# Moving join's scratch into shared tiles, adding a fourth buffer for low parts, and moving one part's token differences to VectorE

## The chip, the cores and the metric

The kernel runs on one core of a Trainium2 chip. The metric is the device time of one execution in microseconds. Three runs of the kernel before took 2678.21, 2679.01 and 2679.69 us; their median, 2679.01 us, is the time that the change is compared with.

## The reference, cut to what matters

A two-layer decoder trunk on 1024 tokens of 1024 channels, all float32. The first layer mixes tokens by the RWKV-7 recurrence with 16 heads of 64 channels, the second by sliding-window attention; each is followed by a squared-ReLU MLP of width 4096. The change touches the first layer alone, and the buffers of the weights of all layers:

```python
xx = token_shift(h) - h                       # differences of neighbouring tokens
xs = h[None] + xx[None] * mu[:, None, None, :]
r, k, v = jnp.einsum('nbtc,ncd->nbtd', xs[:3], w_rkv)   # xw, xa, xg feed the low-rank branches
...
def step(S, inp):                             # wkv7: state S per head, 64 x 64
    r_t, w_t, k_t, v_t, a_t, b_t = inp
    sa = jnp.einsum('bhvk,bhk->bhv', S, a_t)
    S = S * w_t[:, :, None, :] + sa[..., None] * b_t[:, :, None, :] + v_t[..., None] * k_t[:, :, None, :]
    y = jnp.einsum('bhvk,bhk->bhv', S, r_t)
    return S, y
```

## The kernel before, in words

**Products in three matmuls.** Every float32 operand of a large product is split into a high part (a cast to fp32r, ScalarE, L129) and a low part (source less high part, L130, VectorE unless `split` is given another engine). `mm3` then issues three matmuls, L134 to L136. Weights come from HBM into `wr` (5 buffers), their high part goes to `wh` (4 buffers) and their low part to `wl` (3 buffers, `WL = 3`); a [128, 512] tile is 2 KB a partition. In `prod_n` (tokens on the output's partitions) `wl` is read by L135, in `prod_t` (channels there) by L136. A buffer is free for the next weight when the last matmul that reads it is done.

**The first layer's projections** run in three parts of 256, 256 and 512 tokens (`PARTS`). For the first two parts `steps` (L336) takes the differences `dx` of neighbouring tokens, four instructions of [128, 512] on GpSimd (L344); `shifted` then makes each mixed input by one VectorE instruction a channel tile (L353, into one of 3 `relu` buffers), a high part on ScalarE, and a low part, which in the first part is GpSimd's for all 8 tiles (`POOLED`).

**The recurrence** runs in 16 units (8 blocks of 128 tokens by 2 groups of 8 heads), each of two chunks of 64 tokens. A unit is prepared (`prep`, `inner`), two 32 x 32 triangular systems per head are solved on GpSimd (`solve`, L680 and L682) and come back by DMA into `RT`; `join` builds the blocks between them: VectorE transposes `RT`'s blocks into columns 0 to 31 of `XT` (L700), TensorE multiplies (L705), ScalarE copies the product to a tile of its own, `AT` (L707), and TensorE multiplies again (L711). `chunks` then does for each chunk: L743, the right side `pb` (ScalarE, L745), L748, the solve's product L752, its copy into `SV` (VectorE, L754), the state's product L757, the sum `sn` (VectorE, L759), the decayed state (L762 for the next chunk, L763 for `state`) and L766. `AT`, `pb` and `sn` are one buffer each, 1 KB a partition.

**Order.** A scheduler of the framework lays out each engine's instructions from the program's order, priorities and its own cost model; the recurrence is given priority over the products beside it. Each engine then runs its list strictly in order: an instruction that waits holds up everything behind it on its engine. So a buffer count changes the whole list, not only the waits. With the first half's 8 units done, the first half goes through the output projection (`mix_out`) and the MLP, beside which the other 8 units run; attention and the second layer follow.

Of the kernel before, what the change touches and what calls it, by code (L numbers as in the profile page):

```python
# [10 lines left out]
F32 = mybir.dt.float32  # L11
# [3 lines left out]
ALU = mybir.AluOpType  # L15
# [4 lines left out]
P = 128  # L20
# [7 lines left out]
D = 64  # L28
L = 64
TB = 128  # L30
NC = TB // L
GP = 4
# [3 lines left out]
B = 32  # L36
# [7 lines left out]
M2K = 24  # L44
WR = 5
WH = 4
WL = 3
ROWS = 4
STG = 3
RELU = 3  # L50
# [24 lines left out]
class Trunk:  # L75
# [25 lines left out]
    def t(self, pool, tag, shape, dt=F32, bufs=1):  # L101
        return pool.tile(shape, dt, tag=tag, name=self.nm(tag), bufs=bufs)
# [162 lines left out]
    def weight(self, ap, shape, gain=None):  # L265
# [3 lines left out]
        nc.sync.dma_start(raw, ap)  # L269
        hi, lo = self.t(self.mp, "wh", shape, F32R, WH), self.t(self.mp, "wl", shape, F32R, WL)  # L270
        if gain is None:
# [64 lines left out]
    def steps(self, hT, n):  # L336

        self.dx = None
        if n > 256:
            return  # L340
        self.dx = []
        for k in range(0, KT, 2):
            d = self.m2k().bitcast(F32).rearrange("p (k t) -> p k t", t=n)
            self.nc.gpsimd.tensor_tensor(d, hT[0][:, k:k + 2, 0:n], hT[0][:, k:k + 2, 1:], ALU.subtract)  # L344
            self.dx += [d[:, 0], d[:, 1]]

    def shifted(self, hT, i, n):
# [27 lines left out]
    def lora_out(self, W2, u, off, dst, pt):  # L375
# [7 lines left out]
        for o in range(KT):  # L383
            if o % 4 == 0:
                raw = self.t(self.mp, "wr", [P, 512], F32, WR)
                for r0 in (0, 64):
                    nc.sync.dma_start(raw[r0:r0 + 64], W2[:, o * P:o * P + 512])
                wh, wl = self.t(self.mp, "wh", [P, 512], F32R, WH), self.t(self.mp, "wl", [P, 512], F32R, WL)
                nc.scalar.copy(wh, raw)
# [92 lines left out]
    def project(self, pt, hT, left):  # L482
# [44 lines left out]
        for group in groups:  # L527
            for o in group:
                prod(0, o)
                step(small, next(steps))  # L530
# [6 lines left out]
            for o in group:  # L537
                ps = prod(1, o)
                sq = self.t(self.mp, "relu", [P, 512], F32, RELU)[:, :n]
                nc.scalar.activation(sq, ps, AF.Square, scale=self.col('k_k', o))  # L540
                if last is None:
                    s = self.bank()
                else:
                    squares(*last)
                last = (o, sq)
                step(small, next(steps))
# [146 lines left out]
    def join(self, made):  # L693

        nc = self.nc
        AR, BK, RT, EL, bonus, XT, Xs = made
        n = NQ // 2
        sides = [(hp, self.sides(hp)[1].start, self.sides(hp)[2].start) for hp in range(2)]
        for hp, b, k in sides:
            nc.vector.transpose(XT[b:b + B, :, 0:B], RT[k:k + B, hp, :, 0:B])  # L700
        AT = self.t(self.rp, "AT", [P, n, B], F32)
        ps = self.turn().rearrange("p (q i) -> p q i", i=B)
        for q in range(n):
            for hp, b, k in sides:
                nc.tensor.matmul(ps[k + B:k + L, q], XT[b:b + B, q, B:], XT[b:b + B, q, 0:B], start=True, stop=True)  # L705
        for hp, b, k in sides:
            nc.scalar.copy(AT[k + B:k + L], ps[k + B:k + L, 0:n])  # L707
        ps = self.turn().rearrange("p (q i) -> p q i", i=B)
        for q in range(n):
            for hp, b, k in sides:  # L710
                nc.tensor.matmul(ps[k:k + B, q], AT[k + B:k + L, q], RT[k + B:k + L, hp, q, B:], start=True, stop=True)  # L711
        for hp, b, k in sides:
            nc.scalar.copy(RT[k:k + B, hp, :, B:], ps[k:k + B, 0:n])
        return AR, BK, RT, EL, bonus

    def chunks(self, blk, g, made):

        nc = self.nc
        t = lambda tag, shape, bufs=1, dt=F32: self.t(self.rp, tag, shape, dt, bufs)
        pt, t0 = PART[blk]  # L720
        AR, BK, RT, EL, bonus = made
        SV = t("SV", [P, NC, 2, GP, D])
        sides = [(hp, *self.sides(hp)[1:]) for hp in range(2)]
        heads = [(pi, *x) for pi in range(GP) for x in sides]
        dV = self.dV[pt][t0:t0 + TB, g * GH * D:(g + 1) * GH * D]
        for hp, bs, ks in sides:
            for c in range(NC):
                nc.sync.dma_start(SV[ks, c, hp], dV[c * L:(c + 1) * L].rearrange("l (r h d) -> l h r d", h=2, d=D)[:, hp])
            nc.vector.tensor_copy(SV[bs, 0, hp], self.state[g][bs])
        bv = t("bv", [P, NC, GH, D])  # L730
        nc.sync.dma_start(bv[L:].rearrange("l c h d -> l c (h d)"), dV.rearrange("(c l) d -> l c d", l=L))
        nc.gpsimd.tensor_tensor(bv[L:], bv[L:], bonus[L:].unsqueeze(3).broadcast_to([L, NC, GH, D]), ALU.mult)
        y = t("y", [P, GP, NC, L])

        def bank():
            return self.turn().rearrange("p (h d) -> p h d", d=D)[:, 0:GP]

        S = self.state[g]
        for c in range(NC):
            el = EL[:, :, c].unsqueeze(2).broadcast_to([P, GP, D])  # L740
            ps = bank()
            for pi, hp, bs, ks in heads:
                nc.tensor.matmul(ps[ks, pi], AR[:, hp, pi * NC + c, L:], SV[:, c, hp, pi], start=True, stop=True)  # L743
            pb = t("pb", [P, GP, D])
            nc.scalar.copy(pb, ps)  # L745
            py = bank()
            for pi, hp, bs, ks in heads:
                nc.tensor.matmul(py[bs, pi], SV[:, c, hp, pi], AR[:, hp, pi * NC + c, 0:L], start=True, stop=True)  # L748
            nc.scalar.copy(y[:, :, c], py)
            ps = bank()  # L750
            for pi, hp, bs, ks in heads:
                nc.tensor.matmul(ps[bs, pi], RT[ks, hp, pi * NC + c], pb[ks, pi], start=True, stop=True)  # L752
            for hp, bs, ks in sides:
                nc.vector.tensor_copy(SV[bs, c, hp], ps[bs])  # L754
            ps = bank()
            for pi, hp, bs, ks in heads:
                nc.tensor.matmul(ps[bs, pi], BK[:, pi * NC + c, hp], SV[:, c, hp, pi], start=True, stop=True)  # L757
            sn = t("sn", [P, GP, D])
            nc.vector.tensor_tensor(sn, ps, S, ALU.add)  # L759
            if c < NC - 1:  # L760
                for hp, bs, ks in sides:
                    nc.vector.tensor_tensor(SV[bs, c + 1, hp], sn[bs], el[bs], ALU.mult)  # L762
            nc.vector.tensor_tensor(S, sn, el, ALU.mult)  # L763
            py = bank()
            for pi, hp, bs, ks in heads:
                nc.tensor.matmul(py[bs, pi], SV[bs, c, hp, pi], RT[bs, hp, pi * NC + c], start=True, stop=True)  # L766
            nc.vector.tensor_tensor(y[:, :, c], y[:, :, c], py, ALU.add)
        return y, bv
# [355 lines left out]
```

## Time and profile before

| what | value |
|---|---|
| median of three runs | 2679.01 us |
| the profiled execution | 2679.98 us |
| its span, first to last instruction | 2678.3 us |
| TensorE (PE) busy | 2541.7 us, 95% |
| VectorE (DVE) busy | 1700.6 us, 63% |
| ScalarE (ACT) busy | 1306.1 us, 49% |
| GpSimd (POOL) busy | 621.2 us, 23% |
| mean granted TensorE clock | 0.972 of full speed |

The profile is of one execution. Busy shares are means over stages that differ: in the first 800 us the other engines are nearly as busy as TensorE, after that TensorE hardly ever stops. In the rows below, times are in microseconds from the span's start, "L130" is a line of the kernel, and what stands behind an arrow at a row's end is what ended the idle time before it.

### The profile page before, as it was taken

How to read it: one execution, taken by the hardware profiler on the slowest of the kernel's cores; microseconds unless marked ns; L12 is line 12 of the kernel's file. 1: busy time of each engine (PE TensorE's matmuls, PEld its weight loads, DVE VectorE, ACT ScalarE, POOL GpSimd, SP SyncE). 2: the span in 40 equal slices, each digit the busy share in tenths (PEclk: the TensorE clock that was granted, in tenths of full speed). 3: DMA queues.
4: the chain of work that ended last, by engine and by line, in shares of the span. 5: the costliest groups of instructions: out<-in, count | busy, mean ns of one | idle time of the engine just before them, and what ended most of it. 6: DMA issues, size and time to landing. Idle time of an engine off the chain costs nothing.

```text
span 2678.3 us, 43154 instructions
## 1 busy us (share of the span) xinstructions
PE 2541.7 (95%) x15166; PEld 2054.0 (77%) x15166; DVE 1700.6 (63%) x3235; ACT 1306.1 (49%) x2702; POOL 621.2 (23%) x1221
## 2 busy tenths in 40 slices
PE   6978988998889999999999999999999999999999
PEld 4767766766767777777887888888888888888887
DVE  8578778656666666645567885445899644444433
ACT  5555566464444444333455665335666533434342
POOL 6176744740454444420010000001000000000000
PEclk9989989899889999999999999999999999999999
DMA  5656643654644444333424454342446433333332
GB/s 177 196 173 177 184 115 113 179 143 151 177 105 114 120 122 117 109 107 119 140 87 151 126 153 123 95 154 89 138 142 196 123 103 96 121 91 105 96 99 95
DMA packets 440635, 349.64 MB, mean 131 GB/s; under 512 B 97105, under 2 KB 360417, under 8 KB 440417
## 3 DMA queue, kind: packets, MB, share of 16 engines
q1 hardware_dynamic: 423008, 344.77, 43.1%
q10 hardware_dynamic: 17408, 2.10, 0.5%
q8 instruction: 120, 1.97, 0.3%
q14 instruction: 99, 0.80, 0.1%
HBM read 280.71 MB, written 57.67 MB: 126 GB/s over the span
## 4 chain that ended last, share of the span: by engine, by line
PE 50%; DVE 3%; DMA 2%; ACT 1%; issue 1%; SPq 0%; DVEq 0%; ACTq 0%
PE big L134 16%; PE big L135 16%; PE big L136 16%; DMA dS<-sc 1%; DMA row<-dS 1%; DVE wl L130 0%; DVE sc L975 0%; DVE sc L978 0%; DMA wr<-in_mlp_w 0%; PE sm L1001 0%; PE sq L955 0%; PE sm L1002 0%; PE sq L956 0%; PE big L252 0%; SPq L983 0%
## 5 line engine op out<-in xcount | busy, mean ns | idle before, releaser
L129 ACT CAST wh<-wr 128x512 fp32r<-128x512 f32 x741 | 458.0, 620 | 853.4 <-PE big L136 435.5
L130 DVE TENSOR_TENSOR wl<-wr,wh 128x512 fp32r<-128x512 f32 x741 | 527.3, 716 | 474.5 <-issue 223.4
L134 PE MATMUL big<-m2k,wh 128*128 128x512 f32 (+3 forms) x1528 | 578.6, 381 | 12.2 <-ACT m2k L129 4.6
L135 PE MATMUL big<-wl,m2k 128*128 128x512 f32 (+1 forms) x1472 | 578.4, 394 | 9.4 <-DVE wl L130 7.6
L135 PE MATMUL big<-m2k,wh 128*128 128x512 f32 (+2 forms) x1528 | 572.7, 376 | 6.4 <-POOL m2k L130 4.3
L136 PE MATMUL big<-m2k,wl 128*128 128x512 f32 (+2 forms) x1528 | 571.8, 377 | 5.1 <-DVE wl L130 5.1
L136 PE MATMUL big<-wh,m2k 128*128 128x512 f32 (+1 forms) x1472 | 566.9, 392 | 3.0 <-POOL m2k L130 3.0
L134 PE MATMUL big<-wh,m2k 128*128 128x512 f32 (+1 forms) x1472 | 512.1, 394 | 11.3 <-ACT m2k L129 7.7
L134 PEld LDWEIGHTS big<-m2k,wh 128*128 128x128 f32 (+1 forms) x1528 | 292.0, 192 | 76.1 <-issue 6.3
L135 PEld LDWEIGHTS big<-wl,m2k 128*128 128x128 f32 x1472 | 281.3, 191 | 72.2 <-DVE wl L130 13.5
L136 PEld LDWEIGHTS big<-m2k,wl 128*128 128x128 f32 (+1 forms) x1528 | 292.0, 191 | 58.1 <-DVE wl L130 7.7
L135 PEld LDWEIGHTS big<-m2k,wh 128*128 128x128 f32 (+1 forms) x1528 | 291.7, 191 | 57.8 <-POOL m2k L130 7.0
L134 PEld LDWEIGHTS big<-wh,m2k 128*128 128x128 f32 x1472 | 279.9, 191 | 73.0 <-ACT m2k L129 9.1
L136 PEld LDWEIGHTS big<-wh,m2k 128*128 128x128 f32 x1472 | 280.4, 191 | 59.3 <-POOL m2k L130 3.6
L680 POOL TENSOR_TENSOR tmp<-Xs,TT 128x60 f32<-128x60 f32 (+24 forms) x496 | 197.2, 398 | 143.2 <-DMA Xs<-dXs 106.7
L130 DVE TENSOR_TENSOR m2k<-relu,m2k 128x512 fp32r<-128x512 f32 (+1 forms) x200 | 135.1, 678 | 119.6 <-ACT m2k L129 119.2
L682 POOL TENSOR_TENSOR TT<-TT,tmp 128x60 f32<-128x60 f32 (+24 forms) x496 | 195.1, 393 | 37.8
L129 ACT CAST m2k<-relu 128x512 fp32r<-128x512 f32 (+1 forms) x272 | 146.6, 545 | 45.8 <-DVE relu L353 33.4
L322 DVE TENSOR_TENSOR b<-b,big 128x512 f32<-128x512 f32 x192 | 124.7, 680 | 8.8 <-PE big L136 8.2
L223 POOL TENSOR_TENSOR ss<-ss,mhalf 128x4 f32<-128x4 f32 (+1 forms) x10 | 8.9, 888 | 453.8 <-DVE ss L222 453.8
L223 POOL TENSOR_TENSOR qn<-qn,mhalf 128x8 f32<-128x8 f32 x16 | 27.1, 1692 | 373.8 <-DVE qn L222 290.4
L314 ACT ACTIVATE relu<-relu 128x512 f32<-128x512 f32 x128 | 80.9, 633 | 3.5
(229 smaller groups left out, 3089.6 us busy)
## 6 DMA issues: line engine op xcount, KB each, us to landing
wr<-in_mlp_w SPq DMA_DIRECT2D x512, 256.0 KB, 2.7
wr<-in_a_w_rkv SPq DMA_DIRECT2D x144, 256.0 KB, 3.2
ld<-dP SPq DMA_DIRECT2D x16, 1024.0 KB, 6.8
dS<-sc SPq DMA_DIRECT2D x28, 512.0 KB, 2.8
row<-dS SPq DMA_DIRECT2D x112, 128.0 KB, 3.0
dP<-stg SPq DMA_DIRECT2D x64, 128.0 KB, 3.4
AR<-RA SPq DMA_DIRECT2D x32, 256.0 KB, 4.4
Xs<-dXs SPq DMA_DIRECT2D x64, 128.0 KB, 2.7
```

Of the source, the lines that this page charges most:

```text
L129: self.nc.scalar.copy(hi, src)
L130: (engine or self.nc.vector).tensor_tensor(lo, src, hi.bitcast(F32), ALU.subtract)
L134: mm(ps, ah, bh, start=start, stop=False)
L135: mm(ps, ah, bl, start=False, stop=False)
L136: mm(ps, al, bh, start=False, stop=stop)
L223: nc.gpsimd.tensor_tensor(dst, dst, self.mhalf[:, :n], ALU.pow)
L314: nc.scalar.activation(r, r, AF.Square)
L322: nc.vector.tensor_tensor(v, v, ps[tt], ALU.add)
L680: nc.gpsimd.tensor_tensor(v, Xs[:, k:k + 1, k + 1:].broadcast_to([P, m, n]), TT[:, 0:m, k:k + 1].broadcast_to([P, m, n]), ALU.mult)
L682: nc.gpsimd.tensor_tensor(TT[:, 0:m, k + 1:], TT[:, 0:m, k + 1:], v, ALU.add)
```

## The change

Three edits. `WL` goes from 3 to 4. In `steps`, the differences of the first part (`pt` 0) are issued on VectorE and those of the second stay on GpSimd. In `join`, the transposed blocks go to a tile of tag `pb` and `AT` becomes columns 0 to 31 of `XT`, which the transposes no longer use; in `chunks`, `sn` takes the tag `pb` too. So one buffer holds in turn a join's transposed blocks, then right side and sum of each chunk, and two tiles of 1 KB are gone, the size of the new `wl` buffer.

```diff
-WL = 3
+WL = 4
...
-            self.nc.gpsimd.tensor_tensor(d, hT[0][:, k:k + 2, 0:n], hT[0][:, k:k + 2, 1:], ALU.subtract)
+            (self.nc.gpsimd if self.pt else self.nc.vector).tensor_tensor(d, hT[0][:, k:k + 2, 0:n], hT[0][:, k:k + 2, 1:], ALU.subtract)
...
+        TX = self.t(self.rp, "pb", [P, n, B], F32)
         for hp, b, k in sides:
-            nc.vector.transpose(XT[b:b + B, :, 0:B], RT[k:k + B, hp, :, 0:B])
-        AT = self.t(self.rp, "AT", [P, n, B], F32)
+            nc.vector.transpose(TX[b:b + B], RT[k:k + B, hp, :, 0:B])
+
+        AT = XT[:, :, 0:B]
...
-                nc.tensor.matmul(ps[k + B:k + L, q], XT[b:b + B, q, B:], XT[b:b + B, q, 0:B], start=True, stop=True)
+                nc.tensor.matmul(ps[k + B:k + L, q], XT[b:b + B, q, B:], TX[b:b + B, q], start=True, stop=True)
...
-            sn = t("sn", [P, GP, D])
+            sn = t("pb", [P, GP, D])
```

Lines behind L700 stand one or two further down in the changed kernel (L743 is L745 there, L757 is L759).

The first place is VectorE's list at the start of the first part, where the differences (L344) come in. `relu_228` to `relu_290` are the eight mixed inputs of the first low-rank branch, `wl_360` and `wl_372` low parts of the third and fourth weight tile. Before:

```order
L130 TENSOR_TENSOR wl_360<-wr_357,wh_359 128x512
L353 SCALAR_TENSOR_TENSOR relu_228<-m2k_219,vec,b_8_188 128x256
L353 SCALAR_TENSOR_TENSOR relu_242<-m2k_219,vec,b_8_188 128x256
L477 COPY hlast<-b_8_188 128x8
L468 COPY b_367_1551<-hlast 128x8
L353 SCALAR_TENSOR_TENSOR relu_250<-m2k_221,vec,b_8_188 128x256
L353 SCALAR_TENSOR_TENSOR relu_258<-m2k_221,vec,b_8_188 128x256
L353 SCALAR_TENSOR_TENSOR relu_266<-m2k_223,vec,b_8_188 128x256
L353 SCALAR_TENSOR_TENSOR relu_274<-m2k_223,vec,b_8_188 128x256
L353 SCALAR_TENSOR_TENSOR relu_282<-m2k_225,vec,b_8_188 128x256
L353 SCALAR_TENSOR_TENSOR relu_290<-m2k_225,vec,b_8_188 128x256
L130 TENSOR_TENSOR wl_372<-wr_369,wh_371 128x512
```

And now:

```order
L344 TENSOR_TENSOR m2k_219<-b_8_188 128x512
L344 TENSOR_TENSOR m2k_221<-b_8_188 128x512
L130 TENSOR_TENSOR wl_360<-wr_357,wh_359 128x512
L353 SCALAR_TENSOR_TENSOR relu_228<-m2k_219,vec,b_8_188 128x256
L353 SCALAR_TENSOR_TENSOR relu_242<-m2k_219,vec,b_8_188 128x256
L344 TENSOR_TENSOR m2k_223<-b_8_188 128x512
L353 SCALAR_TENSOR_TENSOR relu_250<-m2k_221,vec,b_8_188 128x256
L477 COPY hlast<-b_8_188 128x8
L344 TENSOR_TENSOR m2k_225<-b_8_188 128x512
L130 TENSOR_TENSOR wl_372<-wr_369,wh_371 128x512
L353 SCALAR_TENSOR_TENSOR relu_258<-m2k_221,vec,b_8_188 128x256
L468 COPY b_367_1551<-hlast 128x8
```

The four differences stand among the first mixed inputs, and `wl_372`, which stood behind all eight of them, now stands behind three.

The second place is VectorE's list in the second part, beside the first unit's first chunk. `wl_2212` and `wl_2230` are low parts of two weight tiles, `sn_5501` (now `pb_5501`) is the state sum, `relu_2371` a mixed input. Before:

```order
L130 TENSOR_TENSOR wl_2212<-wr_2209,wh_2211 128x512
L759 TENSOR_TENSOR sn_5501<-sq_5492,states 128x256
L588 MEMSET ec_6152 128x8
L767 TENSOR_TENSOR y_5459<-y_5459,sq_5506 128x4x64
L353 SCALAR_TENSOR_TENSOR relu_2371<-m2k_1678,vec,b_367_1551 128x256
L353 SCALAR_TENSOR_TENSOR relu_2379<-m2k_1676,vec,b_367_1551 128x256
L222 TENSOR_SCALAR ss_2100<-ss_2100 128x2
L130 TENSOR_TENSOR wl_2230<-wr_2227,wh_2229 128x512
```

And now:

```order
L130 TENSOR_TENSOR wl_2212<-wr_2209,wh_2211 128x512
L761 TENSOR_TENSOR pb_5501<-sq_5492,states 128x256
L130 TENSOR_TENSOR wl_2230<-wr_2227,wh_2229 128x512
L588 MEMSET ec_6152 128x8
L353 SCALAR_TENSOR_TENSOR relu_2371<-m2k_1678,vec,b_367_1551 128x256
L769 TENSOR_TENSOR y_5459<-y_5459,sq_5506 128x4x64
L222 TENSOR_SCALAR ss_2100<-ss_2100 128x2
L353 SCALAR_TENSOR_TENSOR relu_2379<-m2k_1676,vec,b_367_1551 128x256
```

`wl_2230` now stands ahead of the two mixed inputs.

The third place is TensorE's list in the third part, at the seventh unit's first chunk; the `sq` tiles are that chunk's products, `big` those of the projections. Rows with + and - are of the list now and of the list before:

```order
+L745 MATMUL sq_7950<-SV_7939,AR_7645 64x64 x8
 L135 MATMUL big_4228<-m2k_4520,wh_4240 64x512
 L136 MATMUL big_4228<-m2k_4519,wl_4241 64x512
-L535 MATMUL big_4501<-relu_4566,ind_114 16x512
-L711 MATMUL sq_7920<-RT_7647,AT_7900 32x32 x16
-L743 MATMUL sq_7950<-SV_7939,AR_7645 64x64 x8
-L748 MATMUL sq_7961<-AR_7645,SV_7939 64x64 x8
+L750 MATMUL sq_7961<-AR_7645,SV_7939 64x64 x8
+L754 MATMUL sq_7971<-pb_7959,RT_7647 64x64 x8
+L759 MATMUL sq_7982<-SV_7939,BK_7646 64x64 x8
+L768 MATMUL sq_7996<-RT_7647,SV_7939 64x64 x8
```

The chunk's four products after the first now stand directly behind one another; before, matmuls of the projections stood between them.

## Rows read from the trace of the kernel before

**Rows 1.** Windows: stretch and length, busy (count) by engine, clock, DMA share, GB/s.

```profile
0.00:60.00 60.00, 38.63 (x154) 26.25 (x155) 50.83 (x94) 31.58 (x71) 41.39 (x57) 1.00 0.53 169
...
200.00:690.00 490.00, 443.24 (x3736) 340.97 (x3736) 349.15 (x707) 281.38 (x619) 238.96 (x489) 0.92 0.54 155
690.00:790.00 100.00, 84.67 (x601) 68.04 (x601) 72.31 (x136) 37.57 (x74) 51.14 (x132) 0.84 0.48 126
790.00:1250.00 460.00, 444.43 (x3465) 353.73 (x3464) 282.13 (x515) 185.83 (x359) 180.84 (x402) 0.99 0.40 112
1250.00:2678.00 1428.00, 1410.85 (x6482) 1165.81 (x6481) 851.07 (x1617) 691.17 (x1401) 45.89 (x43) 1.00 0.39 121
```

**Rows 2.** Waits of TensorE, whole span: total, times, longest.

```profile
...
PE big L135 <- DVE wl L130: 7.6, 11, 1.2
PE big L136 <- DVE wl L130: 5.1, 6, 2.3
...
PE sq L757 <- DVE SV L754: 4.2, 2, 2.5
```

**Rows 3.** Timeline of VectorE in the first part: start, time, instruction [idle before].

```profile
14.93 2.44 DVE L353 SCALAR_TENSOR_TENSOR relu<-m2k,vec,b 128x256 f32<-128x256 f32 x2
17.29 1.00 DVE L477 COPY hlast<-b 128x8 f32<-128x8 f32 x1
...
21.33 2.69 DVE L353 SCALAR_TENSOR_TENSOR relu<-m2k,vec,b 128x256 f32<-128x256 f32 x3 [0.62 <-POOL m2k L130]
25.86 0.69 DVE L130 TENSOR_TENSOR wl<-wr,wh 128x512 fp32r<-128x512 f32 x1 [1.84 <-PE big L136]
26.47 0.88 DVE L353 SCALAR_TENSOR_TENSOR relu<-m2k,vec,b 128x256 f32<-128x256 f32 x2
```

**Rows 4.** Timeline of GpSimd in the first part.

```profile
13.29 4.97 POOL L344 TENSOR_TENSOR m2k<-b 128x512 f32<-128x512 f32 x4 [5.26 <-ACT b L475]
18.23 1.41 POOL L130 TENSOR_TENSOR m2k<-relu,m2k 128x256 fp32r<-128x256 f32 x2
```

**Rows 5.** Timeline of TensorE in the first part.

```profile
19.00 0.48 PE L135 MATMUL big<-m2k,wh 128*64 128x256 f32 x1 [1.85 <-POOL m2k L130]
```

**Rows 6.** Windows, the stretch behind the first part's start.

```profile
28.00:60.00 32.00, 26.50 (x111) 18.64 (x111) 31.76 (x42) 17.71 (x41) 24.17 (x25) 1.00 0.51 149
```

**Rows 7.** Waits of TensorE in the first 100 us.

```profile
PE big L135 <- DVE wl L130: 5.5, 8, 1.2
```

**Rows 8.** Timeline of TensorE, the two longest waits for a low part.

```profile
227.63 0.58 PE L136 MATMUL big<-m2k,wl 128*128 128x256 f32 x1 [2.35 <-DVE wl L130]
...
240.65 0.38 PE L136 MATMUL big<-m2k,wl 128*128 128x256 f32 x1 [1.67 <-DVE wl L130]
```

**Rows 9.** Timeline of VectorE around them.

```profile
225.41 1.38 DVE L353 SCALAR_TENSOR_TENSOR relu<-m2k,vec,b 128x256 f32<-128x256 f32 x2 [3.95 <-POOL m2k L130]
...
226.90 0.68 DVE L130 TENSOR_TENSOR wl<-wr,wh 128x512 fp32r<-128x512 f32 x1
...
238.81 1.21 DVE L586 TENSOR_TENSOR_SCAN ld<-reset,ld 128x512 f32<-128x512 bf16 x1
239.94 0.66 DVE L130 TENSOR_TENSOR wl<-wr,wh 128x512 fp32r<-128x512 f32 x1
```

**Rows 10.** Windows, the stretch of the first of the two waits.

```profile
220.00:240.00 20.00, 16.36 (x137) 14.13 (x135) 15.04 (x25) 10.32 (x26) 18.28 (x35) 0.83 0.72 205
```

**Rows 11.** Timeline of TensorE, the seventh unit's first chunk.

```profile
578.06 0.69 PE L743 MATMUL sq<-SV,AR 128*64 128x64 f32 x16
...
589.38 0.69 PE L757 MATMUL sq<-SV,BK 128*64 128x64 f32 x16
```

**Rows 12.** Timeline of TensorE, the ninth unit's first chunk.

```profile
764.20 0.68 PE L752 MATMUL sq<-pb,RT 64*64 64x64 f32 x16 [0.62 <-ACT pb L745]
767.42 1.12 PE L757 MATMUL sq<-SV,BK 128*64 128x64 f32 x16 [2.53 <-DVE SV L754]
```

**Rows 13.** Timeline of TensorE, the longest wait for a solve.

```profile
750.70 0.31 PE L705 MATMUL sq<-XT 32*32 32x32 f32 x2 [4.77 <-DVE XT L700]
```

## The prediction

> **What bounds the kernel now.** I read the windows by stage first. The reader is to see there that the span falls in two [rows 1]. From 1250 us on, TensorE works 1410.85 of 1428 us at a granted clock of 1.00: 17.2 us are all that any change of buffers could win there. From 790 to 1250 us it rests 15.6 us. Before that the picture is another one: 46.8 us of rest in the stretch from 200 to 690 us, 15.3 us in the next 100, 21.4 us in the first 60, and a clock of 0.92 and 0.84 on top. Whatever this change gives, it gives in the first 790 us, and what it gives there is kept, because afterwards TensorE has work enough to be the bound.
>
> Then I read TensorE's waits over the whole span [rows 2]. The new buffer is for low parts of weights, and TensorE waited for these 7.6 + 5.1 = 12.7 us, in 17 waits. That is the ceiling of the buffer's direct gain. Last I read the timelines of the places where the lists differ.
>
> **Differences on VectorE.** GpSimd took 4.97 us for the four, 1.24 us each, and only then, at 18.23 us, came to the first low part [rows 4]; the matmul that needs it had waited 1.85 us [rows 5]. On VectorE I price one at 0.69 us, as a low part of the same 128x512 with two inputs in SBUF [rows 3]: 4 x 0.69 = 2.8 us more on VectorE. Against this stands what VectorE lost beside GpSimd's four. Two mixed inputs took 2.44 us there; two with GpSimd idle took 0.88 us [rows 3], so 1.6 us come back. The copy of 8 columns that took 1.00 us comes back nearly whole, about 0.8 us. Added and returned work is 2.8 - 2.4 = 0.4 us.
>
> What VectorE waited for goes: 0.62 us for a `relu` buffer that GpSimd held, and 1.84 us in which `wl_372` waited for a buffer still read by TensorE, with mixed inputs ready behind it [rows 3]. In the list now `wl_372` stands behind three mixed inputs and has a buffer of its own. So VectorE comes 1.84 + 0.62 - 0.4 = 2.1 us sooner to the stretch from 28 to 60 us. In that stretch it works 31.76 of 32 us [rows 6]: it is the bound there, not TensorE with 26.50, and 2.1 us sooner at its start is 2.1 us sooner at its end. I take -2.1. The bounds: -3.0 if half of the 1.85 us by which the first low part can come sooner is kept as well, and +1.3 if the differences take what a mixed input took beside GpSimd (1.22 us, so 4 x 0.53 = 2.1 us more) and half of the 2.46 us of waits stay (0.4 + 2.1 - 1.2).
>
> A rule speaks to this edit. The Trainium skill says in SBUF — State Buffer, "Who interferes with whom", that a VectorE instruction with two SBUF inputs contends with a GpSimd instruction that reads SBUF, the second one being blocked until the first is done. Perfetto Trace Analysis, "Optimizing Scalar/DVE Operations", concludes that moving work between these two engines might not help. Here the trace agrees with the first (0.44 us and 1.22 us for the same instruction) and the sum by it would be the port's time alone, 4 x (1.24 - 0.69) = 2.2 us won; the second page's caution would make it nothing.
>
> **The fourth buffer.** Of TensorE's 12.7 us of waits for a low part, 5.5 us lie in the first 100 us [rows 7], nearly all in the stretch where VectorE is the bound; they are counted above and a buffer doesn't shorten them. Of the other 7.2 us, two waits make 2.35 + 1.67 = 4.0 us [rows 8]. VectorE's timeline shows why [rows 9]: at 225.41 us it had stood still for 3.95 us on a mixed input whose buffer GpSimd held, and the low part came behind it at 226.90; at 239.94 the low part came behind a scan of 1.21 us and what stood ahead of that. In the list now, `wl_2230` stands ahead of that mixed input, which a fourth buffer allows. So the first wait goes; the second I take to go by the same step forward. Of the remaining 3.2 us I take a quarter, 0.8. Sum -4.8; bounds 0 (the waits come back on another weight tile) and -7.2.
>
> With the first of these waits the granted clock fell: 0.83 over 20 us [rows 10], so 3.4 us of full speed were lost there, at the lower of the two levels for 6.8 us. Whether one wait of 2.35 us decided it, no row tells; I take half, -1.7, with bounds 0 and -3.4. [...]
>
> **The other side of the new lists.** They move the recurrence too. At the seventh unit's first chunk, 11.3 us lay between the first product and the state's product, filled with projections [rows 11]. Now four products stand directly behind one another, so TensorE must wait for `pb` and then for the copies into `SV`. The ninth unit has the same order before: 0.62 us and 2.53 us [rows 12]. Sum +3.1; bounds +1.0 (the copies alone, if both engines are free at once) and +6.0, if the join ahead of it waits as well. I take +3.0. Elsewhere I compared the work of TensorE that stands between these steps: some units have more, some less, and I take 0, with +-2.
>
> **The shared buffer of `pb`.** The next chunk's right side must wait until VectorE has read the sum for `state`. That instruction stands directly behind the two that make `SV`, and TensorE must multiply with `SV` before ScalarE can write `pb`; VectorE is done first. Behind the waiting ScalarE instruction stand high parts of weights, so a late one would show at once. I take 0; the upper bound is +2.1, if in three of the 32 chunks a low part of 0.69 us [rows 3] has slipped in between. The transposes write as much as before, and columns 0 to 31 of `XT` in the rows that take `AT` are read by nobody else: 0.
>
> **The sum.** -2.1 - 4.8 - 1.7 + 3.0 = -5.6 us. The profiled execution took 2679.98 us, 1.0 us above the median; 2679.98 - 5.6 = 2674.4, and against the median 2679.01 - 5.6 = 2673.4 us. Two per mille, 5.4 us, is what I hold a measurement of this kernel to tell from no change, so this lies on the edge: faster begins below 2673.7.
>
> **Rivals.**
> 1. Given back at the end of the projections. From 690 to 790 us TensorE waits for one unit's solve, 4.77 us at 750 us alone [rows 13], and for that unit's steps [rows 12]. A TensorE that arrives 5 us sooner would wait 5 us longer if the solve doesn't come sooner. For it: the 15.3 us of rest and the clock of 0.84 there [rows 1]. Against it: this unit's data come out of the projections, so its solve starts when these end, and that moves forward with them. It would leave about 1.5 us of gain: 2677.5 us.
> 2. Slower: low parts ahead of the recurrence. With a fourth buffer the scheduler issues low parts earlier, and some now stand on VectorE ahead of the sums and copies of the recurrence. One that has to wait for its buffer holds these up, and TensorE, in order, then waits for `SV` at L757. The price is one or two low parts a chunk, 0.7 to 1.4 us, in the 16 chunks before 790 us; the cover there is the projections' work between the steps, so it decides only where less than 3 us of that is left, as in [rows 12]. At ten such chunks of 1.05 us it is 10.5 us, and with two falls of the clock like that in [rows 10] (3.4 us each) 17.3 us, against 5.6 + 3.0 = 8.6 us won by the rest: 2679.0 + 8.7 = 2687.7 us. For it: waits for `SV` were 4.2 us before, in two places [rows 2], and the third place of the order shows a new one. Against it: VectorE's waits are what the buffer takes away.
> 3. The fourth buffer does nothing, since `wh` has four and both are freed by neighbouring matmuls: the low part can't lead the high part. Then the start's 2.1 us remain: 2676.9 us. Against it: the lists move by whole tiles.
>
> **Chances and range.** The forecast 0.50, rival 1 0.22, rival 2 0.15, rival 3 0.13. Around the forecast the bounds of the terms give 2667 to 2679 as its own range. Below 2673.7 lie about 0.37 of the forecast's half and some of the first and third rivals, together 0.44; within 5.4 us lies 0.42; above 2684.4 about 0.14, which is the second rival. For 8 in 10 I take 2664 (all of the buffer's waits and clock won, nothing lost at the chunks and 2 us won at others: -2.1 - 7.2 - 3.4 - 2 = -14.7) to 2684, which leaves out the most of the second rival and little else.
>
> **What would show it.** Right: the four L344 on VectorE at about 0.7 us each, the first L135 near 17 us instead of 19.00, the end of VectorE's dense stretch about 2 us sooner; no wait for `wl` above 1 us between 220 and 245 us; a wait for `SV` of 1 to 2.5 us at the seventh unit's first chunk. Wrong: L344 above 1 us, waits for low parts as long in sum as 12.7 us, waits for `SV` and `XT` grown by more than those for low parts shrank, or a rest from 690 to 790 us that has grown by what the projections won.

## The result, and the profile after

The changed kernel takes 2640.47 us (median of 4 runs, 2639.18 to 2642.63) against 2679.35 us: a ratio of 0.9852, with a 95% interval of 0.9838 to 0.9866. That is 38.9 us won, where 5.6 us were forecast; the sign was right, the size was not, and half of it came in another place.

The two lines of the page on busy time show of what the gain consists. First before, then after (busy us, share of the span, instructions):

```profile
PE 2541.7 (95%) x15166; PEld 2054.0 (77%) x15166; DVE 1700.6 (63%) x3235; ACT 1306.1 (49%) x2702; POOL 621.2 (23%) x1221
```

```profile
PE 2516.2 (95%) x15166; PEld 2034.4 (77%) x15166; DVE 1693.6 (64%) x3239; ACT 1303.7 (49%) x2702; POOL 629.2 (24%) x1217
```

The spans differ by 2678.3 - 2638.9 = 39.4 us. TensorE executes the same 15166 matmuls in 25.5 us less, so in this pair of executions two thirds of the gain are a higher granted clock; the other 13.9 us are rest. The split is not a steady one. The profiled execution of the changed kernel had a mean clock of 0.983, the other three, just as fast, 0.977 to 0.979, against 0.972 in the profiled execution before. Span times what the mean clock lacks to 1.00 fell by 30 us in the profiled pair, and falls by 14 to 20 us with the other three in its place. The windows after that answer to [rows 1] say where the profiled execution won:

```profile
0.00:60.00 60.00, 41.23 (x162) 28.89 (x163) 51.33 (x98) 33.48 (x74) 37.95 (x54) 1.00 0.54 173
200.00:690.00 490.00, 434.72 (x3686) 334.15 (x3684) 349.63 (x704) 273.72 (x604) 243.75 (x490) 0.93 0.54 156
690.00:790.00 100.00, 87.62 (x671) 70.41 (x671) 74.55 (x143) 44.00 (x88) 58.66 (x153) 0.93 0.47 128
790.00:1250.00 460.00, 458.55 (x3496) 365.87 (x3495) 288.27 (x532) 194.77 (x375) 181.68 (x384) 1.00 0.43 122
1250.00:2638.00 1388.00, 1374.33 (x6324) 1136.95 (x6322) 827.72 (x1579) 673.15 (x1367) 43.39 (x39) 1.00 0.38 120
```

The reader is to see that the rest from 790 to 1250 us is gone: 1.45 us, where it was 15.6, and the clock there went from 0.99 to 1.00. From 690 to 790 us the rest hardly shrank (15.3 to 12.4 us), but the clock rose from 0.84 to 0.93. From 200 to 690 us the rest even grew, from 46.8 to 55.3 us. The stretch that [rows 1] leave out, first before and then after, is the other place of the clock: the same busy time at 0.96 in place of 0.89.

```profile
60.00:200.00 140.00, 119.86 (x734) 99.17 (x732) 95.05 (x171) 78.59 (x181) 62.93 (x98) 0.89 0.63 187
```

```profile
60.00:200.00 140.00, 119.75 (x837) 98.15 (x837) 102.07 (x186) 84.62 (x197) 63.77 (x100) 0.96 0.67 198
```

A second measure of the place needs no clock: ScalarE's copies of the first right side `pb` of the ninth unit and of the sixteenth, two rows before and two after.

```profile
763.81 0.34 ACT L745 COPY pb<-sq 128x256 f32<-128x256 f32 x1
1200.43 0.36 ACT L745 COPY pb<-sq 128x256 f32<-128x256 f32 x1
```

```profile
746.84 0.36 ACT L747 COPY pb<-sq 128x256 f32<-128x256 f32 x1
1164.16 0.36 ACT L747 COPY pb<-sq 128x256 f32<-128x256 f32 x1
```

The changed kernel is 17.0 us ahead at the ninth unit; from there to the sixteenth it takes 417.3 us in place of 436.6, another 19.3 us, though TensorE executes 3341 matmuls in between and executed 3310 before.

What happened in 790 to 1250 us is read from the timelines of one unit's turn between its two chunks. VectorE before (start, time, instruction, [idle before it and what ended it]):

```profile
1021.65 0.42 DVE L759 TENSOR_TENSOR sn<-sq,states 128x256 f32<-128x256 f32 x1
1028.98 0.43 DVE L700 STREAM_TRANSPOSE XT<-RT 32x256 f32<-32x256 f32 x1 [6.91 <-DMA RT<-dTT]
1029.44 0.87 DVE L762 TENSOR_TENSOR SV<-sn,EL 64x256 f32<-64x256 f32 x2
1030.34 0.43 DVE L763 TENSOR_TENSOR states<-sn,EL 128x256 f32<-128x256 f32 x1
1030.69 0.41 DVE L767 TENSOR_TENSOR y<-y,sq 128x256 f32<-128x256 f32 x1
```

TensorE before, at the same place:

```profile
1027.06 0.39 PE L136 MATMUL big<-wh,m2k 128*128 128x512 f32 x1
1029.96 1.09 PE L743 MATMUL sq<-SV,AR 128*64 128x64 f32 x16 [2.52 <-issue]
```

The first chunk's sum `sn` is ready at 1022.07. The two instructions that make `SV` of it for the second chunk need nothing else, but a transpose of the next unit's join stands ahead of them, and it waits 6.91 us for the solve's DMA. TensorE runs out of dense matmuls at 1027.45 and rests 2.52 us for `SV`. The row names no releaser ("issue"). So the wait is in none of the lines of [rows 2]; the view of TensorE's waits has it, whole span, as its second longest, but without the engine that was late:

```profile
PE sq L743 <- issue: 12.2, 6, 2.8
```

VectorE after, at the same unit, behind the second chunk:

```profile
1010.21 0.42 DVE L761 TENSOR_TENSOR pb<-sq,states 128x256 f32<-128x256 f32 x1 [4.12 <-PE sq L759]
1010.66 0.43 DVE L765 TENSOR_TENSOR states<-pb,EL 128x256 f32<-128x256 f32 x1
1011.01 0.41 DVE L769 TENSOR_TENSOR y<-y,sq 128x256 f32<-128x256 f32 x1
...
1013.00 0.88 DVE L701 STREAM_TRANSPOSE pb<-RT 32x256 f32<-32x256 f32 x2
```

The transposes write the one buffer of tag `pb`, so they can't stand ahead of the instructions that still read the second chunk's sum in it. The scheduler now puts them behind, and by then the DMA has landed: no wait. Grouped by line, TensorE's product with `SV` in 790 to 1220 us, before and after (busy us, mean ns | idle before, what ended it):

```profile
L743 PE MATMUL sq<-SV,AR 128*64 128x64 f32 x224 | 11.4, 229 | 12.8 <-issue 12.2
```

```profile
L745 PE MATMUL sq<-SV,AR 128*64 128x64 f32 x224 | 11.1, 228 | 0.0
```

### The profile page after: what moved, and what is told of

Same layout as the page of the kernel before. It is cut to its first block, busy times and chain, and to the rows that moved or that the text cites. A ratio compares the mean times of both kernels' runs of the same rounds, so it can differ in the third digit from the quotient of the medians.

```text
span 2638.9 us, 42800 instructions
## 1 busy us (share of the span) xinstructions
PE 2516.2 (95%) x15166; PEld 2034.4 (77%) x15166; DVE 1693.6 (64%) x3239; ACT 1303.7 (49%) x2702; POOL 629.2 (24%) x1217
## 4 chain that ended last, share of the span: by engine, by line
PE 76%; POOL 7%; DVE 7%; DMA 6%; issue 2%; ACT 2%; SPq 1%; ACTq 0%; POOLq 0%; DVEq 0%
PE big L134 22%; PE big L135 22%; PE big L136 22%; POOL tmp L680 3%; POOL TT L682 3%; DMA ld<-dP 1%; DVE wl L130 1%; PE sm L642 1%; DMA Xs<-dXs 1%; DVE relu L353 1%; DMA dXs<-XT 1%; PE sq L745 1%; PE sq L759 1%; PE sq L754 0%; POOL m2k L130 0%
## 5 line engine op out<-in xcount | busy, mean ns | idle before, releaser
L130 DVE TENSOR_TENSOR wl<-wr,wh 128x512 fp32r<-128x512 f32 x741 | 521.0, 707 | 478.9 <-ACT wh L129 458.6
L134 PE MATMUL big<-m2k,wh 128*128 128x512 f32 (+4 forms) x1528 | 572.4, 377 | 11.9 <-ACT m2k L129 3.9
L135 PE MATMUL big<-wl,m2k 128*128 128x512 f32 (+1 forms) x1472 | 574.0, 391 | 6.1 <-DVE wl L130 6.1
L135 PE MATMUL big<-m2k,wh 128*128 128x512 f32 (+3 forms) x1528 | 571.0, 375 | 6.2 <-POOL m2k L130 3.6
L134 PE MATMUL big<-wh,m2k 128*128 128x512 f32 (+1 forms) x1472 | 558.6, 393 | 15.4 <-ACT m2k L129 12.4
L136 PE MATMUL big<-m2k,wl 128*128 128x512 f32 (+3 forms) x1528 | 567.1, 372 | 4.8 <-DVE wl L130 4.7
L136 PE MATMUL big<-wh,m2k 128*128 128x512 f32 (+1 forms) x1472 | 565.0, 388 | 1.5 <-POOL m2k L130 1.5
L134 PEld LDWEIGHTS big<-m2k,wh 128*128 128x128 f32 (+2 forms) x1528 | 287.4, 189 | 71.5 <-ACT m2k L129 5.6
L134 PEld LDWEIGHTS big<-wh,m2k 128*128 128x128 f32 x1472 | 277.5, 190 | 76.1 <-ACT m2k L129 14.5
L135 PEld LDWEIGHTS big<-m2k,wh 128*128 128x128 f32 (+2 forms) x1528 | 287.7, 188 | 60.7 <-POOL m2k L130 6.9
L136 PEld LDWEIGHTS big<-m2k,wl 128*128 128x128 f32 (+2 forms) x1528 | 287.7, 188 | 55.7 <-DVE wl L130 6.3
L135 PEld LDWEIGHTS big<-wl,m2k 128*128 128x128 f32 x1472 | 279.2, 190 | 66.5 <-DVE wl L130 10.7
L682 POOL TENSOR_TENSOR TT<-TT,tmp 128x60 f32<-128x60 f32 (+24 forms) x496 | 201.0, 405 | 37.8
L314 ACT ACTIVATE relu<-relu 128x512 f32<-128x512 f32 x128 | 80.9, 632 | 3.3
```

The source lines that it names most:

```text
L130: (engine or self.nc.vector).tensor_tensor(lo, src, hi.bitcast(F32), ALU.subtract)
L134: mm(ps, ah, bh, start=start, stop=False)
L135: mm(ps, ah, bl, start=False, stop=False)
L136: mm(ps, al, bh, start=False, stop=stop)
L314: nc.scalar.activation(r, r, AF.Square)
L682: nc.gpsimd.tensor_tensor(TT[:, 0:m, k + 1:], TT[:, 0:m, k + 1:], v, ALU.add)
```

## The experiments

Theory 1: the shared buffer puts the next unit's transposes behind the second chunk's sum, so that VectorE no longer stands for the solve's DMA with `SV` queued behind it. Theory 2: the fourth buffer makes the gain, by other lists. Theory 3: the differences on VectorE make it. The table puts together what decides. "Lost" is worked out from the windows of each trace as length less busy time times granted clock; since the clock is printed with two digits, it is an estimate, good to about 2 us in the two long stretches (200-690 and 790-1220) and to under 1 us in the two short ones. Losses, rests and standings are of one execution each. "Rest at SV" is TensorE's idle time ahead of L743 (L745), "standing" VectorE's wait for the solve's DMA at L700 (L701), both from 790 to 1220 us.

| kernel | ratio (95%) | lost 60-200 | 200-690 | 690-790 | 790-1220 | rest at SV | standing |
|---|---|---|---|---|---|---|---|
| before | 1 | 33.3 | 82.2 | 28.9 | 19.7 | 12.8 | 35.8 |
| after (all three edits) | 0.9852 (0.9838-0.9866) | 25.0 | 85.7 | 18.5 | 1.3 | 0 | 0 |
| e1 join | 0.9888 (0.9876-0.9901) | 35.2 | 80.9 | 19.4 | 0.6 | 0 | 0 |
| e5 blocks shared with `sn` alone | 0.9904 (0.9888-0.9920) | 33.8 | 83.7 | 22.7 | 1.4 | 0 | 3.3 |
| e6 blocks in an own tile | 1.0001 (0.9990-1.0012) | 37.8 | 80.2 | 26.9 | 19.5 | 13.9 | 36.9 |
| e2 after, without sharing | 0.9987 (0.9976-0.9998) | 24.7 | 92.0 | 18.8 | 34.7 | 15.8 | 37.5 |
| e3 differences | 0.9955 (0.9941-0.9970) | 39.0 | 72.8 | 22.4 | 24.7 | 14.5 | 37.6 |
| e4 fourth buffer | 0.9967 (0.9956-0.9979) | 27.0 | 79.7 | 23.9 | 26.1 | 15.9 | 39.1 |
| e7 join, differences | 0.9857 (0.9841-0.9873) | 34.3 | 68.7 | 20.8 | 1.5 | 0 | 0 |
| e8 join, fourth buffer | 0.9847 (0.9834-0.9860) | 24.3 | 81.1 | 24.0 | 0 | 0 | 0 |
| e9 `SV` on GpSimd | 1.0012 (1.0002-1.0022) | 34.0 | 85.3 | 27.4 | 26.1 | 15.8 | 49.3 |
| e12 `SV` on ScalarE | 1.0031 (1.0017-1.0045) | 34.2 | 83.3 | 28.2 | 24.1 | 3.8 | 42.7 |
| e10 join, `WH` 5 | 0.9971 (0.9959-0.9983) | 34.1 | 99.4 | 28.3 | 7.1 | 0 | 1.1 |
| e11 join, `WL` 4, `WH` 5, `WR` 4 | 0.9859 (0.9843-0.9876) | 29.8 | 86.7 | 20.7 | 2.4 | 0 | 0 |

The measure without the clock parts the kernels in the same way. From the ninth unit's first right side to the sixteenth's, the seven kernels whose transposes stand behind the second chunk (after, e1, e5, e7, e8, e10, e11) took 411.5 to 417.8 us, the other seven 436.6 to 448.6 us; e2 and the changed kernel, with the same 3341 matmuls in between, took 445.2 and 417.3 us.

**e1: join's edit alone.** The diff of `join` and `sn` above, with `WL` 3 and the differences on GpSimd.

> The kernel before with one part of the change alone: join's transposed blocks in a tile with the tag of the solve's right side, and the state sum `sn` in the same tag (one buffer); WL stays 3, all differences on GpSimd. Theory 1 (the shared buffer puts the transposes of the next unit behind the second chunk's sum, so that VectorE no longer stands at L700 for the solve's DMA with the second chunk's SV queued behind it): the whole loss from 770 to 1220 us is gone, about 20 us, with some 5 us of units 1 to 7, so about 2652 us; recurrence units of 61 to 62 us in place of 65 to 66; hardly any wait of VectorE at L701 for RT of the solve's DMA in 800 to 1220 us. Theory 2 (fourth buffer for second parts makes the gain, by changed lists): 2676 us or more, units of 65 us. Theory 3 (differences on VectorE): the same as theory 2.

Measured: 2649.35 us beside 2681.16 for the kernel before on the same chip, 1.12% faster, -30 us. Theory 1 held: the loss from 790 to 1220 us is 0.6 us, TensorE has no rest at `SV`, VectorE no wait at L701 there. In the profiled executions it is 3.8 us ahead of the kernel before at the ninth unit and 28.7 us at the sixteenth.

**e2: everything but the sharing.**

```diff
-        TX = self.t(self.rp, "pb", [P, n, B], F32)
+        TX = self.t(self.rp, "AT", [P, n, B], F32)
...
-            sn = t("pb", [P, GP, D])
+            sn = t("sn", [P, GP, D])
```

> The changed kernel with the sharing alone taken out: transposed blocks keep a tile, but of a tag of their own, and `sn` has its own tag again; WL 4 and the first part's differences on VectorE stay. Theory 1: the 20 us from 770 to 1220 us and a part of the earlier gain are lost again, about 2666 us, units of 65 us, and the waits of VectorE at L701 for RT of the solve's DMA are back (6 to 7 us a unit). Theory 2: stays at 2640 to 2646 us with units of 61 to 62 us.

Measured: 2676.90 us, 0.13% faster than before; about 35 us are lost by taking the sharing out, where theory 1 had about 26 (2666 us). The rest at `SV` is back in TensorE's group, 15.8 us:

```profile
L745 PE MATMUL sq<-SV,AR 128*64 128x64 f32 x224 | 13.4, 250 | 15.8 <-issue 15.8
```

The rest is 3 us longer than before the change, and the mean of one matmul rose from 229 to 250 ns, at a clock of 0.96 over the 430 us where before had 0.99.

**e3 and e4: the two other edits alone.**

```diff
-            self.nc.gpsimd.tensor_tensor(d, ...)
+            (self.nc.gpsimd if self.pt else self.nc.vector).tensor_tensor(d, ...)
```

> The kernel before with the first part's token differences on VectorE alone. Theory 1: -2 to -9 us (the first 60 us of the changed kernel), so 2670 to 2677 us, units 8 to 15 still of 65 us. Theory 3 (this edit carries the whole gain): 2645 us.

```diff
-WL = 3
+WL = 4
```

> The kernel before with a fourth buffer for second parts alone. Theory 1: -3 to -8 us, 2671 to 2676 us, from the first 790 us, units 8 to 15 still of 65 us. Theory 2 (the fourth buffer carries the gain): 2645 to 2655 us with units of 61 to 62 us.

Measured: 2668.96 us (-0.45%) and 2672.84 us (-0.33%) beside 2681.16. The fourth buffer came out as expected; the differences gave 12 us, more than the 2 to 9 that I gave them. Neither touches the rest at `SV`; it is 1.7 and 3.1 us longer there. Theories 2 and 3 fell. Where the two gain is told below.

**e5 and e6: what of join's edit does it.** In e5 the blocks share a buffer with `sn` alone, in e6 they have an own one; both have `WL` 3 and the differences on GpSimd.

```diff
+        TX = self.t(self.rp, "sn", [P, n, B], F32)      # e5; "AT" in e6
...
-                nc.tensor.matmul(ps[k + B:k + L, q], XT[b:b + B, q, B:], XT[b:b + B, q, 0:B], ...)
+                nc.tensor.matmul(ps[k + B:k + L, q], XT[b:b + B, q, B:], TX[b:b + B, q], ...)
```

> As the first experiment (WL 3, differences on GpSimd), but the transposed blocks share a one-buffer tag with the state sum `sn` alone; the solve's right side `pb` keeps its own. VectorE's list has the transposes behind the second chunk's L761, L765 and L769 all the same. Theory 1 in its narrow form (what counts is only that the transposes stand behind the second chunk's sum on VectorE, whichever tile forces it): within 4 us of the first experiment's 2649 us, units 8 to 15 of 58 to 62 us. Rival (it is `pb` and `sn` in one buffer, by the order it forces on ScalarE's copy of `pb`): the time of the kernel before, 2675 us or more.

> The kernel before with the transposed blocks in a tile with a tag of its own, `AT` in the freed columns of `XT`; `sn` keeps its tag. VectorE's list has the first transpose between the second chunk's state sum and its SV, as before. Theory 1: no gain, 2676 to 2684 us, units 8 to 15 of 65 to 67 us, VectorE's waits at L701 for RT of 70 to 80 us. Rival (the gain comes from reading the blocks in a tile of 32 columns in place of columns of XT, or from `AT` in `XT`): 2650 to 2660 us.

Measured: 2656.02 us (-0.96%; I had said within 4 us of e1's 2649, it is 7 off, though the intervals of the two ratios overlap) and 2682.95 us (no change). Reading blocks of 32 columns from a tile of their own is worth nothing; a buffer that the second chunk's sum still occupies is worth 26 to 30 us, whichever tile it is shared with. That it acts through the order is read from VectorE's rows; no run moves the transposes without a shared buffer.

**e7 and e8: join's edit with each of the others.**

> Join's edit and the differences on VectorE, WL 3. If the parts add as they were measured alone (join -1.12 %, differences -0.45 %): about 2639 us, as good as the changed kernel with its fourth buffer. If the differences' gain lies in the same waits of 800 to 1220 us that join's edit removes: 2648 to 2652 us.

> Join's edit and the fourth buffer, differences on GpSimd. If the parts add (join -1.12 %, fourth buffer -0.33 %): about 2642 us; with theory 1 the 8 us that the fourth buffer gained before 790 us and lost again in 800 to 1220 us when alone are now kept, so 2636 to 2642 us, near the changed kernel's 2640 us, and the differences on VectorE are then worth nothing on top. If the fourth buffer's gain overlaps with the sharing: 2648 to 2652 us.

Measured: 2641.70 us (-1.43%) and 2639.74 us (-1.53%). Either adds up with join's, and either sum reaches the changed kernel. With join's edit and the fourth buffer the differences on VectorE are worth nothing: 0.9847 without, 0.9852 with them. Nor is the fourth buffer, on top of the other two edits: 0.9857 without, 0.9852 with it.

**e9 and e12: the same rest from the other side.** Join untouched; the two instructions that scale `sn` into the second chunk's `SV` leave VectorE's queue, in e9 for GpSimd, in e12 for ScalarE (8 of 64x64).

```diff
-                    nc.vector.tensor_tensor(SV[bs, c + 1, hp], sn[bs], el[bs], ALU.mult)
+                    nc.gpsimd.tensor_tensor(SV[bs, c + 1, hp], sn[bs], el[bs], ALU.mult)       # e9
...
+                    for pi in range(GP):                                                     # e12
+                        nc.scalar.activation(SV[bs, c + 1, hp, pi], sn[bs, pi], AF.Copy, scale=EL[bs, pi, c:c + 1])
```

> The kernel before, join untouched, with one thing taken from behind the transposes: the second chunk's first SV (L762, the scaling of the state sum) goes from VectorE to GpSimd, where it stands right behind the next solve's last step. The transposes stay between the state sum and what follows it on VectorE and still stand there for the solve's DMA. Theory 1 (TensorE's wait at L743 is the SV queued behind the transposes): GpSimd has SV done some 2 to 4 us before the DMA lands, so that TensorE's idle time at L743 in 790 to 1220 us falls from 12.2 us to 0 to 6 us and the time to 2660 to 2672 us, though the standing at L700 of 6 to 8 us a unit stays. Rival (it is the standing itself, by the other work of VectorE behind it, the dense steps' low parts and L767 above all): no gain, 2678 us or more, also since GpSimd is slower at it.

> The kernel before, join untouched, with the second chunk's first SV (the scaling of the state sum, 2 instructions of VectorE) made by ScalarE in 8 instructions of 64x64; ScalarE has no solve and no wait for its DMA ahead of it. VectorE still stands at L700 for the DMA. The new list of VectorE has the state sum `sn` ahead of the transposes in units 10, 12 and 13, and behind the first transpose in units 11 and 14; so each unit tells something. Theory 1 (TensorE's rests of 790 to 1220 us are the SV, or the sum that it needs, queued behind the transposes): no rest at L743 over 0.5 us in units 10, 12 and 13, one of 2 to 5 us in units 11 and 14; total 2665 to 2676 us. Rival (VectorE's standing costs by whatever else is behind it): the rests, some 12 us in total, are there in all units, at L743 or elsewhere, and the time is 2678 us or more.

Measured: 2684.63 us beside 2680.39 (1.0012) and 2686.34 beside 2678.16 (1.0031), both a little slower; the times that theory 1 gave were wrong. The traces say why. In e9 `SV` stands on GpSimd behind the solve's last step, and so still behind the solve. GpSimd, then TensorE:

```profile
972.96 0.21 POOL L682 TENSOR_TENSOR TT<-TT,tmp 128x8 f32<-128x8 f32 x1
973.12 1.30 POOL L762 TENSOR_TENSOR SV<-sn,EL 64x256 f32<-64x256 f32 x2
```

```profile
973.78 0.27 PE L743 MATMUL sq<-SV,AR 128*64 128x64 f32 x1 [2.98 <-POOL SV L762]
```

In e12 `SV` is early, 893.95 to 896.08 in this unit. But VectorE stands for the DMA all the same, and the sum into `y` is behind it, which empties the PSUM bank that TensorE's next product needs. ScalarE, VectorE, TensorE:

```profile
893.95 2.13 ACT L763 ACTIVATE SV<-sn,EL 64x64 f32<-64x64 f32 x8
```

```profile
900.34 0.43 DVE L700 STREAM_TRANSPOSE XT<-RT 32x256 f32<-32x256 f32 x1 [8.20 <-DMA RT<-dTT]
900.80 0.42 DVE L764 TENSOR_TENSOR states<-sn,EL 128x256 f32<-128x256 f32 x1
901.14 0.69 DVE L130 TENSOR_TENSOR m2k<-relu,m2k 128x512 fp32r<-128x512 f32 x1
901.75 0.41 DVE L768 TENSOR_TENSOR y<-y,sq 128x256 f32<-128x256 f32 x1
```

```profile
902.22 1.12 PE L748 MATMUL sq<-AR,SV 128*64 128x64 f32 x16 [3.44 <-DVE y L768]
```

TensorE's waits of e12 from 790 to 1220 us (line waited for: total, times, longest) repeat it for all units:

```profile
PE sq L748 <- DVE y L768: 8.7, 3, 3.4
PE sq L743 <- ACT SV L763: 3.8, 1, 3.8
PE big L135 <- DVE wl L130: 2.3, 1, 2.3
```

A rest for `SV` stayed in one of the two units whose sum stands behind the transpose; where the sum stands ahead, none was left at `SV`, as theory 1 had it. But the rest came back somewhere else, at the bank of `y` or, once, at a low part. So my theory was too narrow and its rival right in this: it isn't `SV` that the transposes delay but whatever TensorE needs first of VectorE's list behind them. Join's edit moves the transposes behind all of it, and so it works where moving one victim (e12) does not; e9, whose `SV` came to stand behind the solve itself, does not test this. That engines take their instructions in order is also what the Trainium skill says in PSUM — Partial Sum Buffer, "Engine vs sequencer instructions" (the queues of ScalarE, VectorE and GpSimd are strict first in, first out); these rows agree, with 8.20 us of standing and ready work behind it.

**e10 and e11: further buffers.** Join's edit with `WH` 5 (and `WL` 3), and with `WH` 5, `WL` 4 and `WR` 4, to beat both kernels.

> The first experiment (join's edit alone, WL 3) with a fifth buffer for the first parts of weights (WH 5) in place of the fourth for second parts. If any further buffer in the weights' chain relieves the first 200 us: near 2641 us, as with WL 4. If it is the second parts' buffer alone: 2648 to 2652 us.

> Join's edit with WL 4 and WH 5, and one buffer fewer for the raw weights (WR 4). ScalarE waits 65 us before L129 for TensorE to free a `wh` buffer, with VectorE's low parts waiting for ScalarE: if that holds TensorE up, 2630 to 2637 us, below the changed kernel. If loads then come late for want of the raw buffer, 2645 us or more.

Measured: 2672.04 us (0.9971) and 2644.08 us (0.9859). Neither expectation of e10 held, and e11's 2630 to 2637 us did not come either. Neither beats the changed kernel; e10 loses most of join's gain. It keeps it where it arises (7.1 us lost from 790 to 1220 us, no rest at `SV`) and loses 17 us from 200 to 690 us, with its worst stretch near 300 us. The window of e10 there, then that of the kernel before:

```profile
290.00:310.00 20.00, 10.59 (x74) 7.81 (x73) 9.27 (x23) 6.55 (x18) 10.18 (x21) 0.77 0.46 115
```

```profile
290.00:310.00 20.00, 20.00 (x202) 17.36 (x201) 13.67 (x25) 12.59 (x31) 14.33 (x27) 0.96 0.78 216
```

TensorE waits 9.4 us there for one small transpose's input, which ScalarE makes late. Why the fifth buffer leads to that list I have not followed.

## Why the prediction was wrong, point by point

**The stage (wrong).** "Whatever this change gives, it gives in the first 790 us": the 15.6 us of rest from 790 to 1250 us stood in [rows 1], but I took them for TensorE being the bound with enough work. That TensorE hardly ever stops after 800 us, as said with the profile before, holds only from 1250 us on. About half of the gain did come ahead of the ninth unit, 17.0 us, but the other half did not. With the clock of 0.99 this stretch lost 19.7 us up to 1220 us, and 17 to 20 of them came back in every kernel whose transposes stand behind the second chunk, save e10 with 13. What I had not read: the rests of 1.87 to 2.79 us at L743, one a unit in five units, 12.2 us with the sixth, and VectorE's standing of 35.8 us at L700 there. The step of this in the sum is **"The shared buffer of `pb`", which I took at 0 with +2.1 above and no bound below**. I looked at what the sharing holds up (the next right side, nothing) and at columns, but not at where the scheduler must now put the transposes, nor at what they stood in front of: in that stretch VectorE's standing at L700 went from 35.8 us to 0 and TensorE's rest at `SV` from 12.8 us to 0. Alone it is worth -1.12%, 30 us (e1), and taken out of the change it costs about 35 us (e2).

**Differences on VectorE (-2.1 us; right at the start, too small over the kernel).** L344 takes 0.69 us (I said 0.69), and the first L135 begins at 17.29 us (I said near 17; 19.00 in [rows 5]):

```profile
13.37 1.29 DVE L344 TENSOR_TENSOR m2k<-b 128x512 f32<-128x512 f32 x2
...
15.97 0.69 DVE L344 TENSOR_TENSOR m2k<-b 128x512 f32<-128x512 f32 x1
...
18.06 0.68 DVE L344 TENSOR_TENSOR m2k<-b 128x512 f32<-128x512 f32 x1
```

```profile
17.29 0.47 PE L135 MATMUL big<-m2k,wh 128*64 128x256 f32 x1 [0.67 <-POOL m2k L130]
```

TensorE's rest in the first 60 us fell by 2.6 us, but not by this edit alone: in e8 and e10, which lack it, it fell by 1.2 and 1.7 us. What the edit wins up to the second part is read from that part's first difference on GpSimd (L344), at 145.14 us before: it begins 3.5 us sooner in e3 and 4.1 us sooner in e7 than in e1, but in the changed kernel, with the fourth buffer, only 0.7 us sooner than in e8. Alone the edit gave 12 us over the kernel, though, and in e7 8 us on top of join's; the table has them from 200 to 690 us (72.8 and 68.7 us lost against 82.2 and 80.9). With `WL` 4 the same edit loses there (85.7 against e8's 81.1, 92.0 in e2 against e4's 79.7). These are single executions, and why the lists fall better with three buffers no run tells.

**The fourth buffer (place and mechanism wrong; that the size is near is luck).** Forecast -4.8 and -1.7 for the clock, measured -0.33%, 9 us, alone and 0.41%, 11 us, in e8 over e1; in the change as made, over e7, 0.05%, which is no difference. It didn't shorten TensorE's waits for low parts as I priced: they are 10.8 us after, 12.7 before [rows 2]. The two waits of [rows 8] became six of 0.26 to 1.13 us from 218 to 233 us; none above 1.2 us was left there, but the sum is 4.5 us. The gain shows from 60 to 200 us, where every kernel with `WL` 4 lost 24 to 30 us and every one with 3 lost 33 to 39. After this change VectorE hardly waits for TensorE to free a `wl` buffer. Its waits there over the whole span, before and after:

```profile
DVE wl L130 <- issue: 223.4, 105, 5.3
DVE wl L130 <- PE big L135: 109.3, 67, 4.1
DVE wl L130 <- PE big L136: 96.3, 77, 3.4
DVE wl L130 <- ACT wh L129: 20.7, 16, 5.0
```

```profile
DVE wl L130 <- ACT wh L129: 458.6, 256, 5.6
```

Of the 205.6 us for TensorE none is left in the rows after. VectorE doesn't wait less for that: the four rows before make 449.7 us in sum, the one after, for the high part, 458.6. But from 60 to 200 us it does 102.07 us of work instead of 95.05. In the changed kernel this shows as clock, not as rest; in e4 it is both (124.13 us busy at 0.91). Without the sharing half of the lead is lost again: e4 is 22.5 us ahead of the kernel before at the ninth unit and 10.5 us at the sixteenth, with 49 matmuls more in between.

**The clock (mis-sized).** I counted -1.7 us of clock, from one stretch of 20 us. At that place nothing came: from 220 to 240 us the clock rose from 0.83 to 0.91, but from 240 to 260 us it fell from 0.94 to 0.83. Busy time times what the clock lacks to 1.00, before less after, makes 8.4 us from 60 to 200, 5.0 from 200 to 690, 7.4 from 690 to 790 and 4.4 from 790 to 1250 us: 25.2 us, beside the 25.5 us that TensorE was busy less. With two digits of clock the two long stretches are uncertain by some 4 us each, and it is the profiled pair; with the other executions' mean clocks above it is less, still far more than 1.7 us.

**The packed steps of the seventh unit's first chunk (+3.0).** TensorE waited 0.61 us for `SV` there, the row that answers to [rows 11]:

```profile
569.16 1.05 PE L759 MATMUL sq<-SV,BK 128*64 128x64 f32 x16 [0.61 <-DVE SV L756]
```

That is below the bound of +1.0; the term was too dear by more than 2 us.

**The rivals.** Rival 1 had the right picture of 690 to 790 us: the wait for the ninth unit's solve grew from 4.77 [rows 13] to 6.47 us, and a wait of 3.30 us for the second chunk's `SV` came new, while 1.05 us is left of the 2.53 in [rows 12].

```profile
736.94 0.31 PE L707 MATMUL sq<-pb,XT 32*32 32x32 f32 x2 [6.47 <-DVE pb L701]
...
750.67 0.69 PE L759 MATMUL sq<-SV,BK 128*64 128x64 f32 x16 [1.05 <-DVE SV L756]
...
755.41 1.37 PE L745 MATMUL sq<-SV,AR 128*64 128x64 f32 x15 [3.30 <-DVE SV L764]
```

But the clock of 0.93 in place of 0.84 outweighs it. Rival 2, low parts ahead of the recurrence, did not come in the change: e4 and e8 are faster than their counterparts with three buffers, and the changed kernel is as fast as e7. One pair goes the other way: with the differences on VectorE and without the sharing, e2 with four buffers (0.9987) is slower than e3 with three (0.9955); the blocks' own tile, in which they differ too, was worth nothing in e6. TensorE waits 6.6 us for `SV` at the state's product in e2 and 4.5 us in e3, which is too little for the 8 us; the cause is open. Rival 3 is refuted for the buffer alone by e4 and with join's edit by e8; in the change as made its outcome, a buffer worth nothing, came about all the same (e7).

Open: why the differences and the fourth buffer, worth 8 to 12 us each beside join's or alone, give no more together than one of them, and what keeps the clock down from 60 to 200 us with three buffers at a busy time that is the same.

## What to carry to other kernels

Look on every in-order engine for an instruction that stands for a DMA, and read what is queued behind it and which engine needs that: here 4.1 to 7.2 us of standing a unit on an engine that is 63% busy cost the bounding engine 1.9 to 2.8 us a unit in five units, and the wait view of the bounding engine listed it without naming the engine that was late. Where a scheduler chooses the order by its own costs, a shared buffer is an ordering constraint, and it can be worth more than the memory it frees; price where the instruction must now stand, not only who waits for the buffer. Moving one victim out of the queue didn't help (e12), the next one took its place; move the instruction that waits.

## What the runs showed of the hardware that I had not expected

In the profiled pair the same 15166 matmuls took 25.5 us less of TensorE's time, while its rests shrank by only 13.9 us, and executions of the changed kernel that differ by at most 3.5 us in time had mean clocks from 0.977 to 0.983. From 60 to 200 us the busy time is the same to 0.1 us (119.86 and 119.75) at a granted clock of 0.89 and 0.96; how much TensorE rests in a stretch does not tell its clock.
